# The last output column in three pieces of the tokens instead of two

## The chip, the cores and the metric

The kernel runs on one core of one Trainium2 chip. The metric is the device time of one execution in microseconds (us). Three runs of the kernel before took 896.53, 897.54 and 897.56 us, a median of 897.54.

## The reference

One step of a decoder layer, for a prompt of 512 tokens and for 8 samples of one token each, with shared weights. All arrays are float32.

```python
def mix_layer(x, pool_prev, dil_prev, mem_kv, pos0, norm_g, w_in, pool_w, pool_scale,
              dil_q_norm, dil_k_norm, mem_q_norm, w_out):
    z = jnp.einsum('bld,dc->blc', rms_norm(x, norm_g), w_in)
    # columns of z: pooling input and gate, q/k/v of 3 groups of 4 heads, gates, memory q
    ...
    y_pool = pool_mix(u_ext, pos0, pool_w, pool_scale)
    ...
    y_dil = combine_by_denominator(outs, lses).reshape(B, L, DIL_WIDTH).astype(x.dtype)
    ...
    y_mem = mem_attention(q_mem, mem_kv.astype(q_mem.dtype)).reshape(B, L, MEM_WIDTH)
    y = jnp.concatenate([jax.nn.silu(gate_pool) * y_pool,
                         jax.nn.silu(gate_dil) * y_dil,
                         jax.nn.silu(gate_mem) * y_mem], axis=-1)
    x = x + jnp.einsum('blc,cd->bld', y, w_out).astype(x.dtype)
```

The model width is 2048, `w_in` has 7168 columns, and the concatenated `y` has 1536 channels. The change is in the last line, the product with `w_out` and the residual.

## The kernel before

Everything is held with channels on the 128 partitions and tokens along the free dimension: 520 tokens (`NT`), the 512 of the prompt and the 8 samples, in two halves of 260 (`HT`; `SEC` is the list of the two halves, line 548). A block of 128 output channels, called a column here, is one job. It is the sum over blocks of 128 input channels: 16 of them for `w_in`, 12 (`KO`) for `w_out`.

The precision of float32 is reached with three matmuls on operands of the type float32r. Each weight block of 128x128 is split into `whi` (ScalarE rounds it) and `wlo` (VectorE takes the difference), and each activation block into `xh` and `xl`. The products are `whi*xh`, `whi*xl` and `wlo*xh`. `mm` (line 219) issues one matmul; each one carries a 128x128 weight block and up to 260 columns of activations, and the profile shows its weight load as a row of its own on PEld. Attention and transposes use plain float32 matmuls.

A wide job takes a PSUM tile of two banks (`psum_m`, line 152), one bank for each half; two such tiles exist. For an ordinary column the loop goes over the input blocks, then over the three products, then over the two halves (`run_jobs`, line 406). When a column is done, its eviction is put on a list and issued a little later: for an output column VectorE adds the residual `xT` to each half of the PSUM tile (`d_tt`, line 176) and one store of 260 KB writes the column (`o_evac`, line 975).

The instructions are in an order written out by hand, and semaphores between the engines are put in for each tile that is written and read. A planner inside the program keeps a model of each engine's time and decides when side work (attention, norms, pooling) is slipped in between the matmuls. There is no side work left at the end: before the output columns all of it is flushed.

The sixteenth output column is not run by `run_jobs` but by `run_last` (line 463). It has the halves as its outer loop: first all 36 matmuls of the first half (12 blocks times 3 products), then an eviction and a store of this half, and then the same for the second half. Inside the first half, after the first input block, the eviction of the column before is issued (`flush_pend`). The weight splits of the last column stay in their buffers until the end. After `run_last` nothing is left to compute; the program ends when the last store has landed.

Of the kernel before, what the change touches and what calls it, by code (L numbers as in the profile page):

```python
# [23 lines left out]
NT = SEQ + NS  # L24
HT = NT // 2
# [102 lines left out]
def trunk(ctx, tc, nc, I, O):  # L128
# [20 lines left out]
    def row(tag, bufs):  # L149
        return st([P, NT], tag, bufs)  # L150

    def psum_m():
        cnt[0] += 1
        t = ps_m.tile([P, 2, 512], F32, tag="m", name=f"psm_{cnt[0]}")
        ring("psm", 2, t.tensor.name)
        return t
# [19 lines left out]
    def d_tt(out, in0, in1, op):  # L176
        nc.vector.tensor_tensor(out=out, in0=in0, in1=in1, op=op)  # L177
        ck.use("dve", nfree(out) * 0.00104 + 0.08, [in0, in1], [out])
# [40 lines left out]
    def mm(out, lhsT, rhs, start, stop):  # L219
        nc.tensor.matmul(out, lhsT=lhsT, rhs=rhs, start=start, stop=stop)  # L220
        n = nfree(rhs)
        d = 2 * max(0.107, n / 1200.0) if lhsT.dtype == F32 else max(0.107, n * 0.000456 + 0.0015)
        ck.use("pe", d, [lhsT, rhs], [out])
# [9 lines left out]
    def store(out, in_):  # L233
        nc.sync.dma_start(out=out, in_=in_)
        ck.dma(4 * P * nfree(in_), [in_], [])
# [164 lines left out]
    def flush_pend():  # L400
        while pend:
            pend.pop(0)[1]()
# [60 lines left out]
    def run_last(j):  # L463

        t = psum_m()
        xr = xres.pop(j - first_o)
        o = row("tmp", 3)
        for s, (c0, c1) in enumerate(SEC):
            acc = t[:, s, 0:c1 - c0]
            for k in range(KO):  # L470
                whi, wlo = split_t[j, k - k % 4]
                mh, ml = xs(k)
                for n, (w, m) in enumerate(((whi, mh), (whi, ml), (wlo, mh))):
                    mm(acc, w[:, k % 4, :], m[:, c0:c1], k == 0 and n == 0, k == KO - 1 and n == 2)
                if k == 0:
                    flush_pend()
            d_tt(o[:, c0:c1], acc, xr[:, c0:c1], ALU.add)
            store(O["o_y"][j - first_o][:, c0:c1], o[:, c0:c1])
# [69 lines left out]
    SEC = ((0, HT), (HT, NT))  # L548
# [510 lines left out]
    with tc.manual_schedule():  # L1059
# [138 lines left out]
        for gi, seq in enumerate(groups):  # L1198
# [17 lines left out]
            if gi == 0:  # L1216
                run_first(each_first)
                while not flags.get("x"):
                    push()
            elif gi == last_g - 1:  # L1220
                run_jobs(seq, lambda k: split_ready(k))
            elif gi == last_g:
                run_jobs(seq, lambda k: split_ready(KO), before=need_split)
                flush()
                store(O["o_cs"], cs.rearrange("p g b a h -> p (g b a h)"))
                store(O["o_tail"], tail.rearrange("p c t -> p (c t)"))
                load_res(0)
                load_res(1)
            elif gi == len(groups) - 1:
                run_last(seq[0][0])  # L1230
            else:
                run_jobs(seq)
# [100 lines left out]
```

## Time and profile before

| what | value |
|---|---|
| median of 3 runs | 897.54 us |
| profiled execution | 896.3 us, of it a span of 894.6 us |
| PE busy | 882.3 us, 99% of the span, 7208 matmuls |
| VectorE (DVE) busy | 647.3 us, 72% |
| ScalarE (ACT) busy | 388.7 us, 43% |
| one output column on PE | some 8.66 us (stores at 796.07, 804.73, 813.39) |

The span is the time from the first instruction to the last of one profiled execution; the run's time has a little around it. PE is the matmul engine and PEld its weight loads, which overlap with matmuls. Matmuls are pipelined, so that a matmul's row in the timeline (some 0.28 us) is longer than the step from one matmul's start to the next; it is the step that counts. A row with "x8" covers eight instructions, from the first start to the last end.

### The profile page before, as it was taken

Reading aid. Unit: us, or ns where it says so; the run is one execution under the profiler, and the core shown is the slowest. Engines: PE = TensorE matmul, PEld = TensorE weight load, DVE = VectorE, ACT = ScalarE, POOL = GpSimd, SP = SyncE. Lnnn points to the kernel's source line nnn. Section 1 sums busy time; section 2 is a strip of 40 time slices with the busy share of each in tenths; the row PEclk is TensorE's granted clock in tenths of the full one; section 3 lists DMA queues with packets and bytes.
Section 4 is the critical chain, followed back from the end, with each engine's and each line's share of the span. In section 5 each row is a group of like instructions: output and inputs, shape, how many; then the busy total and the mean of one; then the engine's idle time right before and its main releaser. Section 6 shows DMA issues by size and latency. Waiting matters only on the chain.

```text
span 894.6 us, 18350 instructions
## 1 busy us (share of the span) xinstructions
PE 882.3 (99%) x7208; PEld 871.6 (97%) x7208; DVE 647.3 (72%) x1225; ACT 388.7 (43%) x795; POOL 286.6 (32%) x96
## 2 busy tenths in 40 slices
PE   7999999999999999999999999999999999999998
PEld 7999999999999999999999999999999999999998
DVE  7778899975487869988798886888759679422321
ACT  8575565533436334544435353345333615222120
POOL 0132364513346345524155522464334400000000
PEclk9999999999999999999999999999999999999999
DMA  9435355579977866776878699689887776899421
GB/s 333 178 117 204 119 161 184 192 243 320 324 262 261 280 206 218 244 276 244 316 228 307 216 337 339 209 312 301 280 296 254 266 275 206 293 411 325 150 82 48
DMA packets 84518, 219.56 MB, mean 245 GB/s; under 512 B 10696, under 2 KB 24904, under 8 KB 82248
## 3 DMA queue, kind: packets, MB, share of 16 engines
q1 hardware_dynamic: 84432, 218.39, 71.7%
q8 instruction: 56, 0.92, 0.4%
q14 instruction: 30, 0.25, 0.1%
HBM read 200.32 MB, written 106.25 MB: 343 GB/s over the span
## 4 chain that ended last, share of the span: by engine, by line
PE 94%; DVE 4%; issue 1%; DMA 0%; ACT 0%; SPq 0%; DVEq 0%; ACTq 0%
PE psm L220 81%; PE psb L220 12%; DVE wlo L177 1%; DVE sv L200 1%; PE psb L226 1%; DVE tmp L181 1%; DVE sq L181 0%; DVE sk L177 0%; DMA gains<-gains 0%; DVE vt L177 0%; DVE qk L177 0%; DVE smx L196 0%; ACT whi L167 0%; DVE tmp L177 0%; SPq L230 0%
## 5 line engine op out<-in xcount | busy, mean ns | idle before, releaser
L220 PE MATMUL psm<-xh,whi 128*128 128x260 f32 x2088 | 431.9, 287 | 6.6 <-ACT whi L167 6.0
L220 PE MATMUL psm<-xh,wlo 128*128 128x260 f32 x2088 | 423.4, 283 | 2.4 <-DVE wlo L177 2.3
L220 PE MATMUL psm<-xl,whi 128*128 128x260 f32 x2088 | 422.4, 283 | 0.0
L220 PEld LDWEIGHTS psm<-xh,whi 128*128 128x128 f32 x2088 | 324.2, 189 | 13.0 <-ACT whi L167 6.0
L220 PEld LDWEIGHTS psm<-xh,wlo 128*128 128x128 f32 x2088 | 323.0, 189 | 3.2 <-DVE wlo L177 3.2
L220 PEld LDWEIGHTS psm<-xl,whi 128*128 128x128 f32 x2088 | 322.7, 189 | 0.0
L177 DVE TENSOR_TENSOR wlo<-wraw,whi 128x512 fp32r<-128x512 f32 x304 | 248.7, 838 | 50.5 <-ACT whi L167 50.4
L167 ACT ACTIVATE whi<-wraw 128x512 fp32r<-128x512 f32 x304 | 180.2, 622 | 172.4 <-PE psm L220 142.3
L210 POOL PARTITION_ALL_REDUCE sk<-sk x32 | 131.1, 4096 | 175.4 <-DVE sk L177 129.9
L210 POOL PARTITION_ALL_REDUCE sq<-sq x32 | 102.8, 3215 | 128.3 <-ACT sq L167 128.3
L177 DVE TENSOR_TENSOR tmp<-psm,vn 128x260 f32<-128x260 f32 x30 | 11.6, 424 | 89.4 <-PE psm L220 79.0
L167 ACT ACTIVATE sk<-sk,smx 128x256 f32<-128x256 f32 (+1 forms) x64 | 35.4, 553 | 71.0 <-DVE smx L187 37.0
L210 POOL PARTITION_ALL_REDUCE mx<-mx x17 | 46.6, 2741 | 55.0 <-DVE mx L177 54.6
L167 ACT ACTIVATE tmp<-tmp 128x520 f32<-128x520 f32 (+2 forms) x76 | 46.4, 610 | 33.5 <-DVE sq L181 28.7
L167 ACT ACTIVATE sq<-qk 128x520 f32<-128x520 f32 x28 | 17.8, 634 | 71.9 <-DVE qk L177 63.8
L220 PE MATMUL psb<-y,whi 128*128 128x256 f32 x192 | 41.3, 282 | 0.0
L177 DVE TENSOR_TENSOR qk<-psm,rsx 128x260 f32<-128x260 f32 x56 | 21.3, 421 | 22.7 <-PE psm L220 22.7
L220 PE MATMUL psb<-y,wlo 128*128 128x256 f32 x128 | 35.9, 281 | 0.0
L167 ACT ACTIVATE tmp<-sq,eps 128x520 f32<-128x520 f32 (+1 forms) x32 | 22.3, 696 | 28.2 <-POOL sq L210 28.0
L220 PEld LDWEIGHTS psb<-y,whi 128*128 128x128 f32 x192 | 31.6, 188 | 0.0
L200 DVE CUSTOM_DVE_ANT_1 sv<-sv,sk,sy 128x384 f32<-128x384 f32 x32 | 31.1, 1009 | 0.6
L181 DVE SCALAR_TENSOR_TENSOR qk<-qk,gains_r,sq 128x520 f32<-128x520 f32 x28 | 27.7, 988 | 1.0
(129 smaller groups left out, 735.7 us busy)
## 6 DMA issues: line engine op xcount, KB each, us to landing
o_cache<-cache SPq DMA_DIRECT2D x88, 712.0 KB, 7.2
wraw<-w_in SPq DMA_DIRECT2D x208, 256.0 KB, 5.4
o_cache<-cache SPq DMA_DIRECT2D x24, 584.0 KB, 6.0
wraw<-w_out SPq DMA_DIRECT2D x48, 256.0 KB, 5.0
vn<-xT SPq DMA_DIRECT2D x32, 260.0 KB, 5.3
wraw<-w_mem SPq DMA_DIRECT2D x32, 256.0 KB, 4.0
o_zero<-zero SPq DMA_DIRECT2D x6, 1024.0 KB, 7.3
sk<-dks SPq DMA_DIRECT2D x16, 384.0 KB, 5.4
```

The lines of the kernel that those rows point to most:

```text
L167: nc.scalar.activation(out=out, in_=in_, func=func, scale=scale, bias=bias, **kw)
L177: nc.vector.tensor_tensor(out=out, in0=in0, in1=in1, op=op)
L181: nc.vector.scalar_tensor_tensor(out=out, in0=in0, scalar=scalar, in1=in1, op0=op0, op1=op1)
L200: nc.vector.tensor_tensor_reduce(out=out, in0=in0, in1=in1, scale=1.0, scalar=init, op0=op0, op1=op1, accum_out=accum)
L210: nc.gpsimd.partition_all_reduce(t, t, P, op)
L220: nc.tensor.matmul(out, lhsT=lhsT, rhs=rhs, start=start, stop=stop)
L226: nc.tensor.transpose(out, in_, ident)
```

## The change

`run_last` no longer goes through the two halves of the tokens, but through three pieces: tokens 0 to 260, 260 to 390 and 390 to 520. The first piece is the first half, in PSUM bank 0 of the column's tile. The second and the third piece are in bank 1, side by side. Each piece has its own 36 matmuls with all the weight blocks, its own eviction and its own store. `HT` is 260 and `NT` 520.

```diff
         t = psum_m()
         xr = xres.pop(j - first_o)
         o = row("tmp", 3)
-        for s, (c0, c1) in enumerate(SEC):
-            acc = t[:, s, 0:c1 - c0]
+        for c0, c1, s in ((0, HT, 0), (HT, HT + 130, 1), (HT + 130, NT, 1)):
+            acc = t[:, s, c0 - s * HT:c1 - s * HT]
             for k in range(KO):
                 whi, wlo = split_t[j, k - k % 4]
                 mh, ml = xs(k)
```

## Rows read from the trace of the kernel before

**Rows 1.** The page: engines' busy time with share and count, and the chain's shares.
```profile
PE 882.3 (99%) x7208; PEld 871.6 (97%) x7208; DVE 647.3 (72%) x1225; ACT 388.7 (43%) x795; POOL 286.6 (32%) x96
PE 94%; DVE 4%; issue 1%; DMA 0%; ACT 0%; SPq 0%; DVEq 0%; ACTq 0%
```

**Rows 2.** The chain that ended last, from 885 us: start, us, what.
```profile
884.97 1.22 PE psm L220 x10
886.18 0.02 issue
886.20 0.44 DVE tmp L177
886.64 0.04 issue
886.69 4.57 PE psm L220 x36
891.26 0.02 issue
891.28 0.43 DVE tmp L177
```

**Rows 3.** Timeline between the halves: start, us, engine, line, operation, out<-in, form, count, [idle].
```profile
885.75 0.29 PE L220 MATMUL psm<-xl,whi 128*128 128x260 f32 x1
885.76 0.19 PEld L220 LDWEIGHTS psm<-xh,wlo 128*128 128x128 f32 x1
885.88 0.28 PE L220 MATMUL psm<-xh,wlo 128*128 128x260 f32 x1
886.20 0.43 DVE L177 TENSOR_TENSOR tmp<-psm,vn 128x260 f32<-128x260 f32 x1 [3.57 <-PE psm L220]
886.66 0.34 SPq L234 DMA_DIRECT2D o_y<-tmp  x1
886.69 0.19 PEld L220 LDWEIGHTS psm<-xh,whi 128*128 128x128 f32 x1 [0.74 <-DVE tmp L177]
886.69 0.39 PE L220 MATMUL psm<-xh,whi 128*128 128x260 f32 x1 [0.52 <-DVE tmp L177]
886.79 0.19 PEld L220 LDWEIGHTS psm<-xl,whi 128*128 128x128 f32 x1
886.91 0.28 PE L220 MATMUL psm<-xl,whi 128*128 128x260 f32 x1
```

**Rows 4.** The waits of PE: for whom, us in total, times, longest.
```profile
PE psm L220 <- DVE tmp L177: 0.5, 1, 0.5
```

**Rows 5.** Timeline of the end of the program.
```profile
890.84 0.28 PE L220 MATMUL psm<-xl,whi 128*128 128x260 f32 x1
890.96 0.28 PE L220 MATMUL psm<-xh,wlo 128*128 128x260 f32 x1
891.28 0.43 DVE L177 TENSOR_TENSOR tmp<-psm,vn 128x260 f32<-128x260 f32 x1 [4.65 <-PE psm L220]
891.74 0.33 SPq L234 DMA_DIRECT2D o_y<-tmp  x1
```

**Rows 6.** Timeline of an attention head's scores, plain float32, PEld and PE.
```profile
378.04 0.98 PEld L220 LDWEIGHTS psb<-qk,qk 128*128 128x128 f32 x8
378.15 1.05 PE L220 MATMUL psb<-qk,qk 128*128 128x128 f32 x8
```

**Rows 7.** Timeline of four transposes.
```profile
158.38 0.47 PEld L226 LDWEIGHTS psb<-ident,vt 128*128 128x128 f32 x4
158.49 0.60 PE L226 MATMUL psb<-ident,vt 128*128 128x128 f32 x4
```

**Rows 8.** DVE's groups by form: additions that read PSUM (busy us, mean ns | idle).
```profile
L177 DVE TENSOR_TENSOR tmp<-psm,vn 128x260 f32<-128x260 f32 x30 | 11.6, 424 | 89.4 <-PE psm L220 79.0 <-DMA vn<-xT 10.4
L177 DVE TENSOR_TENSOR S<-psb,masks 128x128 f32<-128x128 f32 x4 | 1.1, 282 | 0.0
```

**Rows 9.** Stores of the output columns: all 17, and the DMA issues after 885 us.
```profile
L234 SPq DMA_DIRECT2D o_y<-tmp x17: 332/344/532, 776.7 to 891.7; - x17
DMA to landing us min/median/max: 1.7/2.1/8.2
o_y<-tmp SPq DMA_DIRECT2D x2, 130.0 KB, 1.8
```

**Rows 10.** PE's groups by form: the smallest matmuls with split weights.
```profile
L220 PE MATMUL psb<-y,whi 128*128 128x256 f32 x192 | 41.3, 282 | 0.0
L220 PE MATMUL psb<-y,wlo 128*128 128x256 f32 x128 | 35.9, 281 | 0.0
L220 PE MATMUL psb<-S,whi 128*128 128x256 f32 x48 | 13.5, 282 | 0.0
L220 PE MATMUL psb<-kp,whi 128*128 128x256 f32 x16 | 4.5, 281 | 0.0
```

**Rows 11.** PE at the program's start: timeline, and windows with the granted clock (PEclk).
```profile
7.08 0.65 PE L220 MATMUL psm<-xh,wlo 128*128 128x260 f32 x2
7.52 0.64 PE L220 MATMUL psm<-xh,whi 128*128 128x260 f32 x2
7.96 0.64 PE L220 MATMUL psm<-xl,whi 128*128 128x260 f32 x2
...
core 0: us, PE busy (x) PEld busy (x) DVE busy (x) ACT busy (x) POOL busy (x), PEclk, DMA share, GB/s
0.00:5.00 5.00, 0.00 (x0) 0.00 (x0) 0.00 (x0) 1.53 (x2) 0.40 (x5) 1.00 0.57 163
5.00:10.00 5.00, 3.95 (x20) 3.95 (x21) 3.89 (x7) 4.54 (x9) 0.52 (x4) 1.00 1.02 356
```

## The prediction

> **What bounds the kernel now.** I read the page first. PE is busy for 99% of the span, and the chain that ended last is 94% PE and 4% DVE [rows 1], so the time is PE's time plus what stands between its last matmul and the end. What a changed edit is worth is therefore the change in the length of that one chain, at the place of the edit. The edit touches only the last output column. Everything that is issued before that column's second half is the same, as are the queues up to there: the last column is the last work on PE, and no planner decision comes after it. So I read the chain of waits from 885 us on [rows 2]. It is one file: PE, an eviction by DVE, PE again, an eviction, and then the last store. Nothing runs beside anything, so each nanosecond added there is added to the time.
>
> The timeline shows why PE stops in the middle [rows 3]. The last matmul of the first half starts at 885.88, DVE adds the residual from 886.20 for 0.43 us, and only then, at 886.69, does PE start the second half. The two halves have different PSUM banks, but one tile; PE waited for the DVE that reads this tile (the list of PE's waits has it as 0.5 us, once [rows 4]). The first weight load then stands uncovered: the first matmul starts with it at 886.69 and the second 0.22 us later, where the later ones follow each other in 0.12.
>
> From 886.69 to the end [rows 3, 5]: the second matmul starts 0.22 after the first; 34 more steps to 890.96 take 4.05, so 0.119 each; 0.32 to the start of the eviction at 891.28; 0.43 eviction; 0.03 to the issue of the store at 891.74; 2.86 to the end of the span. Sum 7.91 us. I call this the tail.
>
> **The change part by part.** The first piece keeps its 260 columns. The second half becomes two pieces of 130 columns: 36 matmuls of 260 columns go, 72 of 130 come, so 36 matmuls and 36 weight loads are added, with one eviction and one store.
>
> *Rate of the short matmuls.* This is the term that decides. No row has a 130-column matmul in the one-record form of this loop. What is known: at 260 columns the step is 0.119 us, and each matmul brings its own weights of 128x128, loaded while the one before streams. If streaming alone set the step, 130 columns would take half, 0.060. But the weight load doesn't shrink. Its own pace can be read in three places. After the stop at 886.69, where no matmul is in the way, the second load starts 0.10 us after the first (886.69, 886.79) [rows 3]. Eight 128x128 loads for the attention scores take 0.98 us where one takes 0.19, so they start (0.98 - 0.19)/7 = 0.113 apart, and their matmuls of 128 columns (1.05 - 0.28)/7 = 0.111 apart [rows 6]. Four transposes, again 128 columns with 128x128 weights, take 0.60 where one takes 0.27: 0.11 apart [rows 7]. No pair of load and matmul in these rows comes under 0.10. The rows of 6 and 7 have plain float32 operands, which may stream slower, so alone they would not prove a load limit; the pair of loads at 886.69 has this loop's own operands. I take 0.111 (nearest rows by size), with 0.108 and 0.120 as the ends of this case, 0.060 as the end of all cases from below, and 0.222 from above: one call of a 128-column float32 matmul makes two of those records, since the eight stand for four blocks.
>
> The Trainium skill (TensorE: Matmul & The Clock Gate, section "LDWEIGHTS (loading the stationary operand)") gives a weight load's time as its columns over 1.2 GHz, whatever the contraction: an estimate of 107 ns here, and the pair of loads at 886.69 agrees [rows 3]. By that rule the sum would be 0.3 us less than the one I go by. It speaks against the change, for halving the columns then saves nothing on PE.
>
> *The added stop.* The third piece is in the same PSUM tile as the second, so it waits as the second half waits now: about 0.31 from the last matmul's start to the eviction (a 128-column matmul lasts 0.28 as the 260-column one does [rows 6]), the eviction, 0.06 from its end to the next matmul, and again the uncovered first load. The eviction of 128 columns out of PSUM is in the trace, 282 ns against 424 for 260 [rows 8]; I take 0.28. Not waiting (were the dependency kept by columns) would hide these 0.31 + 0.28 + 0.06 + 0.11 = 0.7 us less one step, some 0.65; the wait of today between two different banks says that it isn't kept by columns.
>
> *The end.* The last eviction is 0.15 shorter. The last store has 65 KB in place of 130. The two stores of 130 KB land 1.8 us after issue (median), and the shortest of all seventeen, mostly of 260 KB, is 1.7 [rows 9]; so size hardly tells, and I take 0.04 off (ends: nothing, and 0.2). The added store of the second piece is issued on SP while PE works on the third piece, lands some 2 us later, and the next eviction comes 4 us later: nothing waits for it. If the pieces ran at 0.060 the third eviction would come 2.8 us later, still behind it. The weights stay in SBUF, so there is no added load.
>
> *Sum.* After: two pieces of 0.22 + 34 x 0.111 + 0.31 + 0.28 = 4.58 make 9.16; 0.06 between them; 0.03; 2.82 to the end: 12.07. Against 7.91 that is +4.2 us. The profiled execution took 896.3 us (span 894.6, so 1.7 lie around it), and would become 900.5. It stands 1.2 below the median of the three runs, 897.54, which is what I add to: 901.7.
>
> **The rivals.**
>
> *Streaming sets the step* (not slower). If the load is hidden behind 130 columns too, the step is 0.060, the first 0.17, the wait for the eviction 0.27: two pieces of 2.76, 0.06, 0.03, 2.82 make 8.43, or +0.5: 898.1. For it: at 260 columns the step is near the streaming time, so no row of this loop shows the load as the bound. Against it: the three places above. A load that is hidden in part, with a step half way between 0.060 and 0.111, 0.085, makes two pieces of 0.195 + 34 x 0.085 + 0.29 + 0.28 = 3.66 and a tail of 10.22, +2.3: 899.8. The place where it decides is the step of the 72 matmuls: under 0.078 the change is within 0.2%. Even with this rate and no stop at all between the pieces, 0.17 + 70 x 0.060 + 0.27 + 0.28 + 0.03 + 2.82 = 7.77, the gain is 0.14 us. So a visible gain is not in reach of any step I can name.
>
> The Trainium skill (same page, section "Back-to-back issue gap") gives some 81 ns for a sustained stream of load and matmul at 128 columns. By that the sum would be about +2.0 us; the 0.111 of rows 6 and 7 is above it, though for float32 operands.
>
> *The short matmul loses the one-pass rate.* If at 130 columns this operand type runs as plain float32 does, each call costs 2 x 0.111 = 0.222 [rows 6]: two pieces of 0.33 + 34 x 0.222 + 0.42 + 0.28 = 8.58, with 2.91 behind them 20.07, +12.2: 909.7. For it: the smallest matmul of this type anywhere in the kernel has 256 columns [rows 10], so nothing shows that a shorter one keeps its rate. Against it: nothing in the rows points to a border.
>
> *The clock falls.* With 130 columns in 0.111 us PE streams for half the time. At the start the matmuls of 260 columns come 0.22 apart, two in 0.44 [rows 11], which is the level of 1.2 GHz, after PE had sat idle for 6 us; the column of the granted clock has 1.00 there all the same, so I go by the steps. In the tail the stop of 0.5 us cost nothing: the steps behind it are 0.12, 2.4 GHz. If the clock fell to the lower level at the beginning of the short pieces and the step went to 0.165, half way to double, the tail would be 2 x (0.33 + 34 x 0.165 + 0.45 + 0.28) + 2.91 = 16.25, +8.3; if it fell half way through, about +6. PE has work in every step here, against an idle start, so I hold it unlikely.
>
> **How the numbers follow.** Load sets the step: 0.66, +4.2 (901.7; its own range 900.4 to 902.5 from the ends 0.108 and 0.120, which are -0.2 and +0.6, and the spread of the runs, 896.53 to 897.56). One-pass rate lost: 0.14, 909.7. Clock: 0.08, 903.5 to 905.8. Streaming 0.07, 898.1; the step between 0.05, 899.8. The range goes up to the rate lost, as the first case with the clock alone holds under 8 in 10, and leaves out the streaming: 900.2 to 910.2. A measurement of this kernel tells about 0.2%, 1.8 us, from no change. Slower by more: 0.66 + 0.14 + 0.08 and half of the step between, and then a little less for the uncertainty of the runs, 0.89. Within: the streaming, the other half and that little, 0.10. Faster: 0.01, for what I have not thought of.
>
> **What would show it.** In the timeline of the changed kernel's tail: matmuls of 130 columns starting 0.11 apart, loads too (0.06: streaming; 0.22 or two records each: rate lost or clock). Two stops of PE for DVE in its waits, the second shorter by 0.15. Evictions of 0.43, 0.28 and 0.28. The third store landing about 1.8 after issue. All rows before 886.6 as now. Wrong in kind I would be if the 72 steps took under 5.6 us together; wrong in size if they took over 9.

## The result and the profile after

The kernel with three pieces took 901.77 us (median of 6 runs, 901.21 to 903.82), the kernel before 897.14 (6 runs, 896.53 to 897.56). The ratio is 1.0054, 95% interval [1.0045, 1.0064]: slower by 4.0 to 5.7 us. Forecast were 901.7 us and +4.2.

The page of the changed kernel: engines' busy time, and the shares of the chain that ended last. They answer to [rows 1]: 36 matmuls more, and 4.8 us more of PE.

```profile
PE 887.1 (98%) x7244; PEld 876.0 (97%) x7244; DVE 647.3 (72%) x1226; ACT 388.6 (43%) x795; POOL 286.9 (32%) x96
PE 92%; DVE 4%; DMA 2%; issue 1%; SPq 1%; ACT 0%; DVEq 0%; ACTq 0%
```

The chain that ended last, changed kernel, from the last columns on (start, us, what; answers to [rows 2]). The one PE piece of 4.57 us and 36 matmuls has become two of 4.25 with 36 each, and between them stands the added stop: an eviction of 0.30, with 0.06 of issue around it.

```profile
888.40 0.44 DVE tmp L177
888.85 0.04 issue
888.89 4.25 PE psm L220 x36
893.14 0.02 issue
893.16 0.30 DVE tmp L177
893.47 0.04 issue
893.51 4.25 PE psm L220 x36
...
897.78 0.29 DVE tmp L177
```

The timeline between the second and the third piece (answers to [rows 3]). Matmuls of 130 columns start 0.11 apart. After the stop the second load starts 0.11 behind the first, and the second matmul 0.16 behind the first.

```profile
892.74 0.28 PE L220 MATMUL psm<-xl,whi 128*128 128x130 f32 x1
...
892.85 0.27 PE L220 MATMUL psm<-xh,wlo 128*128 128x130 f32 x1
893.16 0.29 DVE L177 TENSOR_TENSOR tmp<-psm,vn 128x130 f32<-128x130 f32 x1 [4.33 <-PE psm L220]
...
893.51 0.19 PEld L220 LDWEIGHTS psm<-xh,whi 128*128 128x128 f32 x1 [0.53 <-DVE tmp L177]
893.51 0.33 PE L220 MATMUL psm<-xh,whi 128*128 128x130 f32 x1 [0.39 <-DVE tmp L177]
893.62 0.19 PEld L220 LDWEIGHTS psm<-xl,whi 128*128 128x128 f32 x1
893.67 0.28 PE L220 MATMUL psm<-xl,whi 128*128 128x130 f32 x1
```

The stores after 887 us (KB, median us from issue to landing; answers to [rows 9]).

```profile
o_y<-tmp SPq DMA_DIRECT2D x1, 130.0 KB, 1.8
o_y<-tmp SPq DMA_DIRECT2D x2, 65.0 KB, 1.6
```

I measure the last column from the start of its first matmul to the end of its last eviction: 10.04 us before (881.68 to 891.71), 14.20 after (883.88 to 898.08). So the change costs 4.16 us there; behind the last eviction both programs need 2.88.

The two profiled spans differ by more, 894.6 and 901.0, since the changed kernel's profiled execution, at 903.82 us the longest of its six, was 2.2 us late before the last column. Up to there both kernels issue the same instructions. 0.6 of it stands at the program's start, where the steps of 0.22 us last for the first 21 matmuls instead of the first 15; by 778 us 0.5 of this is left. 1.7 come in there, where PE waits once for an eviction and once for a weight split that VectorE makes behind it (`wlo`); the evictions wait for a load of the residual. From the chains of waits, first of the kernel before, then of the changed one, and the two stops of PE in the changed one's timeline:

```profile
9.03 1.71 PE psb L220 x12
...
774.90 6.15 PE psm L220 x51
```

```profile
9.07 2.27 PE psb L220 x12
...
770.64 7.53 DMA vn<-xT
```

```profile
779.17 0.48 PE L220 MATMUL psm<-xh,whi 128*128 128x260 f32 x2 [0.76 <-DVE tmp L177]
...
780.34 0.51 PE L220 MATMUL psm<-xh,wlo 128*128 128x260 f32 x2 [0.47 <-DVE wlo L177]
```

The edit touches neither place; the other five executions took 901.21 to 902.82.

### The profile page after: what moved, and what is told of

It reads as the page before. It is cut to its first block, busy times and chain, and to the rows that moved or that the text cites. A ratio compares the mean times of both kernels' runs of the same rounds, so it can differ in the third digit from the quotient of the medians.

```text
span 901.0 us, 18425 instructions
## 1 busy us (share of the span) xinstructions
PE 887.1 (98%) x7244; PEld 876.0 (97%) x7244; DVE 647.3 (72%) x1226; ACT 388.6 (43%) x795; POOL 286.9 (32%) x96
## 4 chain that ended last, share of the span: by engine, by line
PE 92%; DVE 4%; DMA 2%; issue 1%; SPq 1%; ACT 0%; DVEq 0%; ACTq 0%
PE psm L220 80%; PE psb L220 11%; DVE wlo L177 1%; DMA vn<-xT 1%; DVE sv L200 1%; PE psb L226 1%; DMA wraw<-w_in 0%; DVE sk L177 0%; DVE sq L181 0%; DVE tmp L181 0%; DMA gains<-gains 0%; DMA o_mem<-vt 0%; SPq L234 0%; DVE tmp L177 0%; SPq L230 0%
## 5 line engine op out<-in xcount | busy, mean ns | idle before, releaser
L220 PE MATMUL psm<-xh,whi 128*128 128x260 f32 (+1 forms) x2100 | 435.2, 287 | 7.8 <-ACT whi L167 6.1
L220 PE MATMUL psm<-xh,wlo 128*128 128x260 f32 (+1 forms) x2100 | 426.7, 283 | 2.9 <-DVE wlo L177 2.8
L220 PE MATMUL psm<-xl,whi 128*128 128x260 f32 (+1 forms) x2100 | 425.6, 283 | 0.0
L177 DVE TENSOR_TENSOR tmp<-psm,vn 128x260 f32<-128x260 f32 (+1 forms) x31 | 11.7, 415 | 95.2 <-PE psm L220 94.0
```

## The experiments

The theory: the step of a short matmul is the pace of its weight load, 0.112 us for 128 weight columns, so a piece of 130 columns costs PE nearly what one of 260 costs (4.25 against 4.57). The rivals: 130 columns of this operand type stream at half the rate of 260, which would make a step of 0.11 to 0.12 too (260 take 0.119); and, for the smaller term, a stop that isn't made by the shared tile. All figures of "the column" are measured as above.

**Half the weight columns** (64 of 128 in the second and third piece).

```diff
-            acc = t[:, s, c0 - s * HT:c1 - s * HT]
+            n = 64 if s else P
+            acc = t[0:n, s, c0 - s * HT:c1 - s * HT]
...
-                    mm(acc, w[:, k % 4, :], m[:, c0:c1], k == 0 and n == 0, k == KO - 1 and n == 2)
+                    mm(acc, w[:, k % 4, 0:n], m[:, c0:c1], k == 0 and i == 0, k == KO - 1 and i == 2)
...
```

> As the changed kernel, but the second and third piece load 64 of the 128 weight columns, and so compute, evict and store 64 of the 128 output channels of these tokens; the other half of these outputs is left out. The moving columns stay 130. Theory, the weight load sets the step: it falls from 0.112 to the streaming of 130 columns, 0.06 to 0.07; the measure from 9.99 to 6.6 to 7.1; time some 3 us below the changed kernel. Rival, 130 moving columns of this type stream at half the rate (130 at 1.2 GHz are 0.108): the step stays 0.11, measure 9.99. If the load has a fixed part the step lies between.

897.87 us (10 runs; ratio to the kernel before 1.0008, [0.9999, 1.0017]), the column 10.59, and 6.38 from the first piece's last matmul, under the 6.6 to 7.1 that were expected. The step lies in its range; the expectation left out that the uncovered first load (0.055 against 0.108) and the wait for the eviction (0.26 against 0.31) shrink too. The timeline of the third piece's start:

```profile
890.02 0.27 PE L220 MATMUL psm<-xh,whi 128*64 128x130 f32 x1 [0.38 <-DVE tmp L177]
890.07 0.14 PEld L220 LDWEIGHTS psm<-xl,whi 128*64 128x64 f32 x1
890.13 0.23 PE L220 MATMUL psm<-xl,whi 128*64 128x130 f32 x1
...
890.19 0.22 PE L220 MATMUL psm<-xh,wlo 128*64 128x130 f32 x1
```

With the same 130 moving columns the step falls to 0.062, about half of the 0.119 at 260. The half-rate rival is out, and the load of 128 columns is what makes 0.112. After the stop, two loads of 64 columns start 0.055 apart and two of 128 columns 0.108, so that no fixed part of the load shows. The column is 3.61 shorter than the changed kernel's, out of the 4.16 that the change costs.

**Half the weight columns at 260 moving columns.** The same edit with the two halves of before.

```diff
-        for c0, c1, s in ((0, HT, 0), (HT, HT + 130, 1), (HT + 130, NT, 1)):
+        for c0, c1, s in ((0, HT, 0), (HT, NT, 1)):
```

> The kernel before with two halves, but the second half loads 64 of the 128 weight columns and computes, evicts and stores 64 of the 128 output channels; the other half of these outputs is left out. It asks what sets the step of 0.119 at 260 columns. If streaming does: 0.116 to 0.119, no change, since the load was hidden. If the load has a part in it (0.112 of it are the load's own pace): the step falls towards the pure streaming time of 260 columns, 0.110 or less, and the second half gets some 0.3 us shorter.

896.36 us in its one execution. The timeline after the stop:

```profile
886.57 0.34 PE L220 MATMUL psm<-xh,whi 128*64 128x260 f32 x1 [0.52 <-DVE tmp L177]
...
886.75 0.28 PE L220 MATMUL psm<-xl,whi 128*64 128x260 f32 x1
886.87 0.28 PE L220 MATMUL psm<-xh,wlo 128*64 128x260 f32 x1
```

The step stays 0.119 (median of 35): at 260 columns streaming sets it, and the load is hidden. The column is 9.95, 0.09 less; 0.05 of this is the first step after the stop, 0.175 in place of 0.227, as the uncovered load is half as long. This is one execution, without an interval.

**Four pieces of 130**, the change twice.

```diff
-        for c0, c1, s in ((0, HT, 0), (HT, HT + 130, 1), (HT + 130, NT, 1)):
+        for c0, c1, s in ((0, 130, 0), (130, HT, 0), (HT, HT + 130, 1), (HT + 130, NT, 1)):
```

> All 520 tokens in four pieces of 130: the change twice. Theory (36 more loads at 0.112 and one more stop for each split): another 4.2 us, 8.3 to 8.5 above the kernel before, some 905.6 us, ratio 1.0094. Rival, the price is that of the program's end (a late last store, the wait after the shorter piece) and not of each short matmul: as the changed kernel, +4.5, or less than +6.

904.77 us against 897.10, ratio 1.0091, [1.0077, 1.0105]. The column is 18.33, +8.29 over before, nearly twice 4.16. By the times it is 7.7 over before (6.9 to 9.4 by the interval), where 8.3 to 8.5 were expected; behind its last eviction the profiled execution needs 2.58, 0.3 less than the changed kernel's. Its chain repeats the same 4.25 and 0.30:

```profile
886.58 4.25 PE psm L220 x36
...
890.86 0.30 DVE tmp L177
...
891.21 4.25 PE psm L220 x36
```

The price belongs to each split, and not to the program's end.

**The third piece in a tile of its own.**

```diff
-        for c0, c1, s in ((0, HT, 0), (HT, HT + 130, 1), (HT + 130, NT, 1)):
-            acc = t[:, s, c0 - s * HT:c1 - s * HT]
+        need("psb")
+        t3 = psum_b()
+        for c0, c1, acc in ((0, HT, t[:, 0, 0:HT]), (HT, HT + 130, t[:, 1, 0:130]),
+                            (HT + 130, NT, t3[:, 0:130])):
```

> The third piece writes a PSUM tile of its own; the second piece stays in bank 1 of the column's tile. Measure: from the start of the first piece's last matmul to the end of the last eviction (5.83 us before, 9.99 after). Load theory with a wait made by the shared tile: PE goes from the second to the third piece without a stop, 0.55 of stop and 0.055 of uncovered load go, 9.39; run time some 0.6 below the kernel with three pieces. Rival, PE waits for the eviction whatever tile it writes: 9.99, no change. The step of the short matmuls stays at 0.112 in both.

901.48 us, ratio to before 1.0046, [1.0031, 1.0061]; by the times alone it can't be told from the changed kernel. Its trace tells: from the first piece's last matmul to the end 9.39, the column 13.60. The chain has no eviction between the pieces any more:

```profile
888.45 4.24 PE psm L220 x36
892.69 4.03 PE psb L220 x36
```

So the stop goes when the third piece has its own tile, and it is 0.60 of the 4.16. With the 3.61 that went with half the weight columns this makes 4.21, so the two together are the price. Here the bank changes along with the tile; the next kernel tells the two apart.

**The two halves in tiles of their own**: the kernel before without its stop.

```diff
-        for s, (c0, c1) in enumerate(SEC):
-            acc = t[:, s, 0:c1 - c0]
+        need("psb")
+        t2 = psum_b()
+        for c0, c1, acc in ((0, HT, t[:, 0, 0:HT]), (HT, NT, t2[:, 0:HT])):
```

> Two halves as in the kernel before, the second in a PSUM tile of its own. If the stop between the halves is the shared tile's: the matmuls of 260 columns run on with 0.12 steps, the measure goes from 5.83 to 0.12 + 35 x 0.119 + 0.32 + 0.43 = 5.04, and the time to some 0.8 us under the kernel before (ratio 0.9991, at the border of what a measurement tells). Rival, the stop is not the tile's: 5.83 and no change.

896.28 us (11 runs) against 897.10 (21 runs), ratio 0.9993, [0.9984, 1.0002]: the interval still touches no change. The trace shows the 0.8: 5.03 from the first half's last matmul to the end, the column 9.24, and PE without a wait for DVE in it:

```profile
869.94 17.32 PE psm L220 x144
887.25 4.29 PE psb L220 x36
```

Its halves were in different banks before too, so it is the tile that they share, and not the bank, that makes the stop. It is the shortest last column of all that ran.

**Other sizes: 196 and 64 columns.**

```diff
-        for c0, c1, s in ((0, HT, 0), (HT, HT + 130, 1), (HT + 130, NT, 1)):
+        for c0, c1, s in ((0, HT, 0), (HT, HT + 196, 1), (HT + 196, NT, 1)):
```

> The second half in pieces of 196 and 64 columns, all else as in the changed kernel. Theory, the weight load sets the step as long as the columns stream in less: 0.112 for the 196 columns and 0.112 for the 64, the two pieces equally long but for the evictions (about 0.36 and 0.23). Rival, short matmuls of this type stream at half the rate and the load is hidden: 0.163 for 196 and 0.055 for 64. From the first piece's last matmul to the end of the last eviction 10.0 by the theory, about the same by the rival; only the steps tell them apart.

902.23 us in its one execution. At 196 the step is 0.111 and at 64 it is 0.112, as the theory has it, but only until 895.0. Then it is 0.213 to 0.215 for the last eight matmuls, and the whole is 10.94 instead of 10.0: this expectation missed. The timeline at the start of the 196-column piece and at the place of the fall, and the windows of the two pieces (the column before the last two is the granted clock):

```profile
887.28 0.36 PE L220 MATMUL psm<-xh,whi 128*128 128x196 f32 x1 [0.52 <-DVE tmp L177]
...
887.48 0.27 PE L220 MATMUL psm<-xl,whi 128*128 128x196 f32 x1
...
887.59 0.27 PE L220 MATMUL psm<-xh,wlo 128*128 128x196 f32 x1
...
894.93 0.30 PE L220 MATMUL psm<-xh,wlo 128*128 128x64 f32 x1
895.04 0.40 PE L220 MATMUL psm<-xh,whi 128*128 128x64 f32 x1
...
895.26 0.40 PE L220 MATMUL psm<-xl,whi 128*128 128x64 f32 x1
```

```profile
887.30:891.30 4.00, 4.00 (x36) 4.00 (x36) 0.00 (x0) 0.00 (x0) 0.00 (x0) 1.00 0.10 33
894.00:895.00 1.00, 1.00 (x11) 1.00 (x10) 0.00 (x0) 0.00 (x0) 0.00 (x0) 1.00 0.00 0
896.00:897.00 1.00, 1.00 (x6) 1.00 (x5) 0.00 (x0) 0.00 (x0) 0.00 (x0) 0.50 0.00 0
```

The clock went from its upper level (1.00, 2.4 GHz) to the lower (0.50, 1.2 GHz) while PE ran 64-column matmuls without a gap.

The first steps after a stop bear the theory out in a second way. Each is the distance of the first two loads and a rest. The loads are 0.108 apart for 128 weight columns and 0.055 for 64. The rest is 0.02 at 64 moving columns, 0.058 at 130, 0.091 at 196 and 0.119 at 260, and it is the same at 130 and at 260 with 64 weight columns. So the rest goes with the moving columns alone, and one can read it as their streaming: uncovered, load and streaming add up, and in the loop the longer of the two sets the step.

Two more kernels ask whether it is the short columns or the stop ahead of them that lowers the clock.

**196 and 64, the 64 in a tile of its own**, so without the stop (the edit is that of the third piece in its own tile, with these sizes: `t[:, 1, 0:196]` and `t3[:, 0:64]`).

> Pieces of 196 and 64 again, where the granted clock fell in the last piece 3.0 us after its start and the step went from 0.112 to 0.213. Here the 64-column piece has a PSUM tile of its own, so that no stop of PE lies between the pieces. Theory, the short columns are what lowers the clock: it falls again inside the last piece, steps of 0.213 at its end. Rival, the stop of 0.7 us between the pieces does it: the clock stays at its upper level, all steps 0.112, and the tail is some 1.5 us shorter than with the stop.

901.07 us in its one execution. The clock falls all the same, at 893.5, to 0.50 in the windows from 894 on; the last eleven matmuls have steps of 0.213. From the first piece's last matmul 10.54. So the fall doesn't need the stop.

```profile
894.00:895.00 1.00, 1.00 (x6) 1.00 (x6) 0.00 (x0) 0.00 (x0) 0.00 (x0) 0.50 0.00 0
```

**64 first, then 196.**

```diff
-        for c0, c1, s in ((0, HT, 0), (HT, HT + 130, 1), (HT + 130, NT, 1)):
+        for c0, c1, s in ((0, HT, 0), (HT, HT + 64, 1), (HT + 64, NT, 1)):
```

> The 64-column piece comes second and the 196-column piece third, both in the column's tile. Theory, the short columns lower the clock: it falls towards the end of the second piece or behind it, and part of the 196 columns' steps are 0.2 until it rises again; the whole tail 10 to 14 us, against 10.0 at the upper level throughout. Rival, the fall belongs to the end of the program or to the stop before the last piece and not to the columns: the second piece keeps 0.112 and the third too.

13.16 from the first piece's last matmul; 905.24 us in its one execution. Its chain, and a window of the 196 columns and one behind them:

```profile
888.17 4.22 PE psm L220 x36
...
892.70 7.44 PE psm L220 x36
```

```profile
893.00:894.00 1.00, 1.00 (x6) 1.00 (x6) 0.00 (x0) 0.00 (x0) 0.00 (x0) 0.50 0.15 33
900.00:901.00 1.00, 0.12 (x2) 0.00 (x0) 0.36 (x1) 0.00 (x0) 0.00 (x0) 1.00 0.00 0
```

Here the 64 columns keep 0.112 to their end, and the clock falls at 892.5, in the stop behind them. It is down when the 196 columns begin, they run at 0.213 and not at 0.111, and it comes back only for their last steps from 899.4 on. So the fall goes with the 64-column piece, in it or right behind it, wherever it stands. Each of these three kernels ran once, and the mean granted clock of the execution is 0.996 or 0.997 in all three. In every run of the kernels with 130-column pieces it is 0.999 or 1.000. Why 64 columns lose the clock and 130 don't stays open, and no size between them ran.

## Why the prediction was right

**The step of the short matmuls**, the term that decides: 0.111 forecast from the float32 rows, 0.112 measured (median of 35 in each piece). That the load makes it was argued then from a pair of loads 0.10 apart, and is shown now by halving the weights. That the float32 rows had the right number is luck in part. In the trace of the kernel before, plain float32 matmuls of 512 columns start (1.88 - 0.59)/3 = 0.43 apart, also with 128x128 weights:

```profile
253.88 1.88 PE L220 MATMUL psb<-S,vmem 128*128 128x512 f32 x4
```

A quarter of this, for 128 columns, is 0.107 (an estimate), so the 0.111 of rows 6 and 7 can be the streaming of plain float32 as well as a load. Of the three places only the pair of loads spoke for the load.

By the Trainium skill (TensorE: Matmul & The Clock Gate, section "LDWEIGHTS (loading the stationary operand)") the estimate was 107 ns, 5 below; the trace agrees at the upper level of the clock (0.108 to 0.112), and not at the lower, where loads start 0.213 apart.

**The first step after a stop** was put at 0.22 and is 0.166 and 0.164. I added a whole step to the uncovered load; what follows the load is only the streaming of 130 columns (0.108 + 0.058). That is 0.11 too much in the sum.

**From the last matmul to the eviction**: 0.31 forecast, 0.312 and 0.311. **Eviction**: 0.28 forecast from 128 columns, 0.294 and 0.293. **Eviction to the next matmul**: 0.06 forecast, 0.054. **The end**: 2.82 from the store's issue to the end of the span forecast, 2.85 measured. The smaller store did land sooner than I took it to (1.6 against 1.8, where I took 0.04 off), but the end of the program used this up. "Size hardly tells" was a wrong reading: the shortest landing, 1.7, is that of a 130 KB store itself, while the 260 KB stores of the last columns ahead of it take 2.0 to 2.1. The sum from the second piece's first matmul to the end was 12.07, and is 901.0 - 888.9 = 12.1. That it fits so closely is luck: the 0.11 too much of the first steps is made up by 0.05 in the other steps, 0.03 in the evictions and 0.03 at the end.

**The wait** of the third piece was forecast at some 0.65 in its full price, and taking it away gave 0.60. (The four terms there add up to 0.76, not 0.7; less one step this is 0.65.)

**The rivals.** Streaming sets the step: out at 128 weight columns; its price was right, though, for with 64 weight columns the step is 0.062, where 0.060 was forecast, and the column is 0.55 over before, where +0.5 was. A load that is hidden in part: out, no step of the 130 columns behind the first is under 0.108. The Trainium skill's 81 ns for a stream at 128 columns (same page, "Back-to-back issue gap") is not seen with these operands: 0.112. One-pass rate lost: out, neither 130, 196 nor 64 columns show it. The clock falls: not at 130 columns, for the windows of the changed kernel's two short pieces and of the last three of the four-piece kernel have 1.00 (three of them below); at 64 it does, and there my price was too low (0.165, "half way to double"): the load's pace follows the clock, 0.112 to 0.213. I had held the fall unlikely because PE has work in every step; the 64-column kernels show that this is no protection.

The windows of the changed kernel's second and third piece, then of the four-piece kernel's last piece:

```profile
888.80:893.50 4.70, 4.24 (x36) 4.09 (x36) 0.33 (x2) 0.00 (x0) 0.00 (x0) 1.00 0.08 28
893.50:898.10 4.60, 4.24 (x36) 4.09 (x36) 0.29 (x1) 0.00 (x0) 0.00 (x0) 1.00 0.05 14
```

```profile
895.80:900.10 4.30, 4.23 (x36) 4.09 (x36) 0.00 (x0) 0.00 (x0) 0.00 (x0) 1.00 0.05 15
```

**The signs.** The matmuls and loads 0.11 apart, the two stops of the last column (0.52 and 0.39) and the evictions came as listed; the third store landed 1.6 after its issue, not 1.8. "All rows before 886.6 as now" did not hold: the instructions are the same, but the profiled execution was 2.2 us late by then.

**The number.** That 901.7 and the measured 901.77 agree to 0.1 is luck. The kernel before came out at 897.14, 0.4 under the 897.54 that I added to, and the difference of the medians is 4.6, 0.4 over the forecast 4.2. The medians differ by 4.6 us and the column by 4.16. The remaining half microsecond is within the interval of the ratio, 4.0 to 5.7, and the trace of one execution can't settle whether it is more than the spread seen ahead of the column.

## What to carry to other kernels

Before the moving side of a matmul is split, look for the pace of its weight load: find two loads with no matmul in the way, and compare their distance with the step. Here pieces of 64, 130 and 196 columns all cost 0.111 to 0.112 per matmul while the clock is up, so that a shorter last piece lengthens the chain by 36 loads (4 us) to save 0.14 of an eviction and 0.2 of a store's landing, which the end of the program didn't give back. If the end of a program is to be shortened, look first for a stop that a shared tile makes: a tile of its own for the second half took 0.8 us out of the column, and its trace shows no price for it. By the times, the gain is too small to be told from no change.

## What the runs showed that I had not expected

The granted clock of PE fell to half while matmuls of 64 moving and 128 weight columns followed each other without a gap (two kernels), or in the stop right behind such a stretch (one kernel), and it didn't with 130 moving columns. The profile's busy share of PE is no sign of it: the windows show PE busy for 1.00 of 1.00 us at either level. And a weight load takes twice as long at the lower level (0.213 against 0.112), so a kernel of such short matmuls pays double once the clock is down.
